# One-core MoE transformer layer: final norm spread over the last expert, one chunk for gate and up, routing lists as stationary operand

## The chip, the core and the metric

The kernel runs on one core of one Trainium2 chip. The metric is the device time in microseconds (us). Before the change it is 2897.74 us, the median of 3 runs (2894.93 to 2900.19). The engines are TensorE (PE; PEld is its weight load), VectorE (DVE), ScalarE (ACT), GpSimd (POOL) and SyncE (SP), which issues most transfers.

## What is computed

A transformer layer of 1024 tokens of width 1024: modulated RMS norm, attention, Fourier and pooling mixers, merge, output projection; then a mixture of 16 experts in which each expert chooses 128 tokens, and a final RMS norm. The change touches only the end:

```python
affinity = jax.nn.softmax((h @ w_router).astype(jnp.float32), axis=-1)
gates, idx = lax.top_k(jnp.swapaxes(affinity, 1, 2), cap)        # 16 experts, cap = 128 tokens
xg = h[b_idx, idx]
a = jnp.einsum('becd,edf->becf', xg, w_gate)                     # d = 1024, f = 2816
u = jnp.einsum('becd,edf->becf', xg, w_up)
y = jnp.einsum('becf,efd->becd', jax.nn.silu(a) * u, w_down) * gates[..., None]
out = jnp.zeros_like(h).at[b_idx, idx].add(y)
...
x = x + g2 * out
return rmsnorm(x, final_norm_g)
```

## The kernel before

Everything up to the experts stays as it is. The function `moe` (L1071) streams the weights of 16 experts, 34.6 MB each, through SBUF. The 2816 hidden columns are cut into chunks of 512, the last (c = 5) of 256. The unit of work is a **half**: half of one chunk's gate, up or down matrix, 1 MB (0.5 MB in the last chunk). An expert is 36 halves, in the order gate, up, and the down of the chunk before: g0 g1 u0 u1 | g0 g1 u0 u1 d0 d1 | ... The list `halves` holds them all, and one loop runs over them. In its turn j it does, in this order:

- what was put into `before[j]`;
- `products(j)`: 12 matmuls of 512 columns (three for each 128-deep slice, `mm3`, L70). In the last chunk gate and up have 12 matmuls of 256 columns for each half, and down has 6 of 512;
- after u1, `gated` (L1205): the product of Silu(gate) and up on DVE; its transposes (`turn`, L1209) are put two turns later;
- `split(j + 4)` (L1167): a cast of the raw half on ACT (L67) and a subtraction on DVE (L68) give the high and low parts in a `whl` buffer. There are four of these, so the cast waits for the products of turn j;
- `load(j + 15)` (L1154): SP issues the transfer into the next of 12 raw buffers, once the split that read that buffer is done;
- after g1, `silu` (L1201) on ACT.

The order on PE, ACT and DVE is this program's order, written out by hand; each engine works through its queue in order, and so do SP and POOL.

In the third chunk (c = 2) of an expert the next expert's tokens are chosen. `choose_hot` (L1095) builds a 0/1 matrix on DVE after g0; before u1 `choose_rows` (L1104) multiplies it, as stationary operand, with a table of four columns (L1109, 8 matmuls), and DVE copies token numbers and gate out of PSUM (L1112, L1118, L1119). POOL then gathers the rows (L1114), and PE transposes them in c = 4. The result of an expert is scaled (`scaled`, L1218) and added into `xacc` in DRAM by a scatter on POOL (L1226) in the next expert's second chunk.

The last expert is not scattered. `final` (L1304) loads the 8 blocks of 128 tokens of `xacc`, builds a 0/1 matrix `hot`, splits the scaled result, adds it into the blocks with 32 matmuls, squares each block on ACT (L1339), takes the reciprocal root (`rstd`, L103), multiplies and stores 8 blocks (L1350).

Of the kernel before, what the change touches and what calls it, by code (L numbers as in the profile page):

```python
# [19 lines left out]
D = 1024  # L20
# [18 lines left out]
class Kernel:  # L39
# [63 lines left out]
    def rstd(self, ss, pool, tag):  # L103
# [967 lines left out]
    def moe(self, upto):  # L1071
        nc, io = self.nc, self.io
        NR = RING
        with ExitStack() as st:
# [3 lines left out]
            ring_pool("wraw3", 5)  # L1078
            ring_pool("wraw4", NR - 8 - 3)
# [5 lines left out]
            cnt = [0]  # L1085

            class Ring:
                def tile(_, *a, **k):
                    cnt[0] += 1
                    return raws[(cnt[0] - 1) % NR].tile(*a, **k)  # L1090

            ring = Ring()
# [11 lines left out]
            def choose_rows(ex, held=None):  # L1104
# [3 lines left out]
                for c in range(CB):  # L1108
                    nc.tensor.matmul(tp[:, :4], hot[:, c], self.tv[:, c, e], start=c == 0, stop=c == CB - 1)  # L1109
# [42 lines left out]
            raw, W = {}, {}  # L1152

            def load(j):  # L1154
# [3 lines left out]
                f0, n = chunks[c]  # L1158
                if w == "w_down":
                    v, k, cols = io[w][e][f0:f0 + n], n // 256, D  # L1160
                else:
                    v, k, cols = io[w][e][:, f0:f0 + n], KT // 2, n
                v = v.rearrange("(k p) c -> p k c", p=128)[:, k * s:k * s + k]
                raw[j] = ring.tile([128, 2048], F32, name="wraw"), k, cols
                nc.sync.dma_start(raw[j][0][:, :k * cols].rearrange("p (k c) -> p k c", c=cols), v)
# [14 lines left out]
            def products(j, ex):  # L1180
                w, e, c, s = halves[j]
                n = chunks[c][1]
                hl = W.pop(j)
# [10 lines left out]
                if s == 0:  # L1194
                    ex.h[w] = psg.tile([128, 512], F32, name=w)
                for k in range(KT // 2):
                    kk = s * (KT // 2) + k
                    self.mm3(ex.h[w][:, :n], ex.xT[:, 0, kk], ex.xT[:, 1, kk], hl[:, 0, k], hl[:, 1, k],
                             kk == 0, kk == KT - 1)

            def silu(ex, n):  # L1201
                ex.a = sp.tile([128, 512], F32, name="a")
                nc.scalar.activation(ex.a[:, :n], ex.h["w_gate"][:, :n], AF.Silu)

            def gated(ex, n):  # L1205
                nc.vector.tensor_mul(ex.a[:, :n], ex.a[:, :n], ex.h["w_up"][:, :n])
                ex.ready = ex.a
# [33 lines left out]
            for j in range(9):  # L1241
                load(j)
            with self.pool("first", 1, side="right") as fp:

                ex = expert(0)
                choose_rows(ex, fp.tile([128, 6144], I32, name="first"))
            ring_pool("wraw5", 3)
            for j in range(9, NR):
                load(j)
# [6 lines left out]
            for j in range(NR, NR + AHEAD - 1):  # L1256
                load(j)
# [3 lines left out]
            for j, (w, e, c, s) in enumerate(halves):  # L1261
# [6 lines left out]
                if s == 1 and w == "w_up":  # L1268
                    gated(ex, n)
                    if c == last:  # L1270
                        split(j + AHEAD - 1)

                        put(after, j + 1, ("first", lambda ex=ex, c=c, n=n: turn(ex, c, n)))
                    else:
                        put(before, j + 2, lambda ex=ex, c=c, n=n: turn(ex, c, n))
# [4 lines left out]
                if (w, c, s) != ("w_up", last, 0):  # L1280
                    split(j + AHEAD)
                load(j + AHEAD + NR - 1)
# [3 lines left out]
                if s == 1 and w == "w_gate":  # L1286
                    silu(ex, n)
# [10 lines left out]
            for b in range(2):  # L1298
                scaled(ex, b)
            order.close()  # L1300
# [134 lines left out]
```

## Time and profile before

| | |
|---|---|
| median of 3 runs | 2897.74 us |
| the profiled execution's own time | 2896.28 us |
| its span, first to last instruction | 2894.5 us |
| PE busy | 2774.9 us (96%) |
| DVE busy | 2038.0 us (70%) |
| ACT busy | 1686.1 us (58%) |
| HBM read and written | 710 and 71 MB |

The experts take from about 1320 us to 2860 us, 95.4 us each; `final` takes the rest. In a profile row of the timeline the first number is the start in us from the span's start, the second the time to the end of the last instruction of the row; x8 means that eight instructions in a row are merged. In square brackets stands how long the engine sat idle before and who released it. PE records overlap: a matmul's pace is the distance between starts.

### The profile page before, as it was taken

The numbers are of one execution on the slowest core, as the hardware profiler recorded it, in microseconds if no ns is written. First come the engines' busy times: TensorE is split into PE (matmuls) and PEld (weight loads), VectorE is DVE, ScalarE is ACT, GpSimd is POOL, SyncE is SP. The second block draws the span as 40 slices with busy tenths as digits, with TensorE's granted clock in tenths as the row PEclk, the third lists the DMA queues.
The fourth block names the chain that finished last, engine by engine and source line by source line (L and its number), as shares of the span: only waits on it lengthen the run. The fifth ranks groups of instructions, "written<-read, shape, count | busy, mean of one in ns | idle before, by whom it ended". The sixth has DMA issues, their size and how long they took to land.

```text
span 2894.5 us, 36071 instructions
## 1 busy us (share of the span) xinstructions
PE 2774.9 (96%) x13607; PEld 2303.0 (80%) x13607; DVE 2038.0 (70%) x2412; ACT 1686.1 (58%) x2005; POOL 279.6 (10%) x436
## 2 busy tenths in 40 slices
PE   7999999999999889996999999999999999999996
PEld 3888888888788787875888888888888888888885
DVE  4423231235578773478889888998899889988997
ACT  5412121212068781244777777777777777777775
POOL 1111000000144320000000000000000000000000
PEclk9999999999999999997999999999999999999998
DMA  8434231224968748557999999999999999999994
GB/s 249 175 124 152 74 131 55 95 82 154 299 173 207 179 135 285 179 171 270 337 365 387 369 376 369 383 372 374 368 382 375 375 370 379 376 374 368 371 385 184
DMA packets 346351, 783.54 MB, mean 271 GB/s; under 512 B 17288, under 2 KB 61008, under 8 KB 346048
## 3 DMA queue, kind: packets, MB, share of 16 engines
q1 hardware_dynamic: 326272, 713.48, 70.0%
q0 software_dynamic: 19664, 67.60, 6.9%
q8 instruction: 107, 1.75, 0.3%
q14 instruction: 68, 0.56, 0.1%
q10 hardware_dynamic: 240, 0.16, 0.0%
HBM read 710.37 MB, written 70.80 MB: 270 GB/s over the span
## 4 chain that ended last, share of the span: by engine, by line
PE 45%; DMA 3%; DVE 3%; ACT 3%; issue 1%; DVEq 0%
PE y L72 5%; PE y L74 5%; PE y L73 5%; PE w_gate L74 5%; PE w_gate L72 5%; PE w_gate L73 5%; PE w_up L72 5%; PE w_up L74 4%; PE w_up L73 4%; DMA wraw<-in_w_up 3%; PE tp L1212 1%; ACT whl L67 1%; DVE whl L68 1%; ACT xT L1138 1%; DMA wraw<-in_w_down 0%
## 5 line engine op out<-in xcount | busy, mean ns | idle before, releaser
L68 DVE TENSOR_TENSOR whl<-wraw,whl 128x2048 fp32r<-128x2048 f32 (+1 forms) x656 | 1292.6, 1997 | 216.2 <-ACT whl L67 213.9
L67 ACT CAST whl<-wraw 128x2048 fp32r<-128x2048 f32 (+1 forms) x660 | 1091.1, 1671 | 414.0 <-PE y L74 124.9
L73 PE MATMUL mm<-hT,whl 128*128 128x512 f32 x768 | 301.4, 393 | 1.6 <-DVE hT L278 1.6
L72 PE MATMUL mm<-hT,whl 128*128 128x512 f32 x768 | 300.3, 392 | 1.5 <-ACT hT L272 1.5
L74 PE MATMUL mm<-hT,whl 128*128 128x512 f32 x768 | 301.2, 392 | 0.0
L74 PE MATMUL w_gate<-whl,xT 128*128 128x512 f32 (+1 forms) x768 | 286.9, 374 | 2.8 <-DVE xT L1143 2.8
L72 PE MATMUL w_gate<-whl,xT 128*128 128x512 f32 (+1 forms) x768 | 289.5, 377 | 0.0
L72 PE MATMUL w_up<-whl,xT 128*128 128x512 f32 (+1 forms) x768 | 288.7, 376 | 0.0
L73 PE MATMUL w_gate<-whl,xT 128*128 128x512 f32 (+1 forms) x768 | 286.3, 373 | 0.0
L74 PE MATMUL w_up<-whl,xT 128*128 128x512 f32 (+1 forms) x768 | 286.0, 372 | 0.0
L73 PE MATMUL w_up<-whl,xT 128*128 128x512 f32 (+1 forms) x768 | 285.6, 372 | 0.0
L72 PE MATMUL y<-whl,aT 128*128 128x512 f32 x704 | 282.4, 401 | 0.0
L74 PE MATMUL y<-whl,aT 128*128 128x512 f32 x704 | 275.5, 391 | 0.0
L73 PE MATMUL y<-whl,aT 128*128 128x512 f32 x704 | 275.2, 391 | 0.0
L72 PEld LDWEIGHTS mm<-hT,whl 128*128 128x128 f32 x768 | 145.0, 189 | 37.3 <-ACT sg L534 5.2
L73 PEld LDWEIGHTS mm<-hT,whl 128*128 128x128 f32 x768 | 145.2, 189 | 31.9 <-DVE hT L278 2.1
L74 PEld LDWEIGHTS mm<-hT,whl 128*128 128x128 f32 x768 | 145.4, 189 | 30.0
L74 PEld LDWEIGHTS w_gate<-whl,xT 128*128 128x128 f32 x768 | 145.1, 189 | 29.0 <-DVE xT L1143 3.5
L73 PEld LDWEIGHTS w_gate<-whl,xT 128*128 128x128 f32 x768 | 145.4, 189 | 24.8
L74 PEld LDWEIGHTS w_up<-whl,xT 128*128 128x128 f32 x768 | 144.8, 188 | 25.6
L72 PEld LDWEIGHTS w_gate<-whl,xT 128*128 128x128 f32 x768 | 145.3, 189 | 24.7
L73 PEld LDWEIGHTS w_up<-whl,xT 128*128 128x128 f32 x768 | 144.9, 189 | 24.1
(354 smaller groups left out, 4327.9 us busy)
## 6 DMA issues: line engine op xcount, KB each, us to landing
wraw<-in_w_gate SPq DMA_DIRECT2D x160, 1024.0 KB, 11.4
wraw<-in_w_up SPq DMA_DIRECT2D x160, 1024.0 KB, 9.2
wraw<-in_w_down SPq DMA_DIRECT2D x160, 1024.0 KB, 12.0
wraw<-in_w_in SPq DMA_DIRECT2D x28, 1024.0 KB, 5.5
wraw<-in_ada_w SPq DMA_DIRECT2D x24, 1024.0 KB, 7.5
wraw<-in_w_gate SPq DMA_DIRECT2D x32, 512.0 KB, 12.4
wraw<-in_w_up SPq DMA_DIRECT2D x32, 512.0 KB, 9.4
wraw<-in_w_down SPq DMA_DIRECT2D x32, 512.0 KB, 6.3
```

Of the source, the lines that this page charges most:

```text
L67: self.nc.scalar.copy(hi, src)
L68: (eng or self.nc.vector).tensor_sub(lo, src, f(hi))
L72: mm(out, lh, rh, start=start, stop=False, **kw)
L73: mm(out, lh, rl, start=False, stop=False, **kw)
L74: mm(out, ll, rh, start=False, stop=stop, **kw)
L1138: nc.scalar.activation(ex.xT[:, 0, kk], tp[:, cs], AF.Identity, bias=B, scale=A)
L1212: nc.tensor.transpose(tp[:, 128 * k:128 * k + 128], ex.ready[:, 128 * k:128 * k + 128], self.ident)
```

## The change

Three edits. (1) The lists: `choose_list` multiplies with the table as stationary operand (4 columns) and the 0/1 matrix as moving operand (128 columns); DVE copies the 4 x 128 result to SBUF; one turn later `choose_rows` transposes it on PE and goes on as before. (2) The last chunk's gate and up columns lie side by side: two halves named "both" of 512 columns, 34 halves in an expert instead of 36; Silu and `gated` follow at once. (3) The final norm: with H halves in all, five of the 12 raw buffers are kept, from turn H-27 on, for the norm's gain and the 1024 rows of `xacc`; squares, two `rstd` of four blocks each, scalings in place and stores of all rows are spread over turns H-22 to H-4 of the last expert. The last expert gathers its own 128 rows of `xacc`; after its last matmul it adds them, norms these rows alone and scatters them over `out`. The last two halves are multiplied together, first all of one half of the columns, then the other. `final` is gone. The five kept buffers are one pool now (`wraw4`).

```diff
-    def rstd(self, ss, pool, tag):
+    def rstd(self, ss, pool, tag, eps=None):
...
+        if eps is not None:
+            nc.scalar.activation(s, ss, AF.Sqrt, scale=1.0 / D, bias=eps)
         nc.vector.tensor_scalar(v, ss, 1.0 / D, EPS, op0=ALU.mult, op1=ALU.add)
-        nc.scalar.sqrt(s, v)
+        if eps is None:
+            nc.scalar.sqrt(s, v)
...
-            ring_pool("wraw3", 5)
-            ring_pool("wraw4", NR - 8 - 3)
+            ring_pool("wraw3", 1)
+            ring_pool("wraw4", NR - 7)
...
-            def choose_rows(ex, held=None):
+            def choose_list(ex):
                 e, hot = ex.hot
                 tp = pst.tile([128, 512], F32, name="tp")
                 for c in range(CB):
-                    nc.tensor.matmul(tp[:, :4], hot[:, c], self.tv[:, c, e], start=c == 0, stop=c == CB - 1)
+                    nc.tensor.matmul(tp[:4, :128], self.tv[:, c, e], hot[:, c], start=c == 0, stop=c == CB - 1)
+                ex.list = sp.tile([4, 128], F32, name="list", bufs=1)
+                nc.vector.tensor_copy(ex.list, tp[:4, :128])
+
+            def choose_rows(ex, held=None):
+                tp = pst.tile([128, 512], F32, name="tp")
+                nc.tensor.transpose(tp[:, :4], ex.list, self.ident[:4, :4])
...
-                    todo = [("w_gate", c), ("w_up", c)] + [("w_down", c - 1)] * (c > 0) + [("w_down", c)] * (c == last)
+                    todo = [("both", c)] if c == last else [("w_gate", c), ("w_up", c)]
+                    todo += [("w_down", c - 1)] * (c > 0) + [("w_down", c)] * (c == last)
...
+            def finish_load(i):
+                t = fin[i] = ring_tile(keep=True)
...
+                    nc.sync.dma_start(t.rearrange("p (s d) -> p s d", s=2),
+                                      self.xacc[256 * (i - 1):256 * i].rearrange("(s p) d -> p s d", s=2))
...
+            def finish_square(i):
...
+                nc.scalar.activation(fin[0][:, D:], fin_row(i), AF.Square,
+                                     accum_out=fin["ss", i // 4][:, i % 4:i % 4 + 1])
...
+            def finish_store(i):
+                x = fin_row(i)
+                nc.vector.scalar_tensor_tensor(x, x, fin["r", i // 4][:, i % 4:i % 4 + 1], fin[0][:, :D],
+                                               op0=ALU.mult, op1=ALU.mult)
+                nc.sync.dma_start(io["out"][128 * i:128 * i + 128], x)
...
+            H = len(halves)
+            FIN = H - 12
...
+            late = {H - 29: [lambda ex: finish_rows(ex)]}
+            for i, lag in enumerate((22, 21, 20, 19, 17, 15, 14, 12)):
+                late.setdefault(H - lag, []).append(lambda ex, i=i: finish_square(i))
+            late.setdefault(H - 18, []).append(lambda ex: finish_rstd(0))
+            late.setdefault(H - 10, []).append(lambda ex: finish_rstd(1))
+            for i, lag in enumerate((17, 15, 14, 13, 9, 8, 7, 4)):
+                late.setdefault(H - lag, []).append(lambda ex, i=i: finish_store(i))
+
+            def stream(j):
+                if j < FIN:
+                    load(j)
+                elif j < FIN + 5:
+                    finish_load(j - FIN)
+                else:
+                    load(j - 5)
...
+                if s == 1 and w == "both":
+                    silu(ex, ex.h[w][:, :n])
+                    gated(ex, ex.h[w][:, n:2 * n])
+                    put(after, j + 1, ("first", lambda ex=ex, c=c, n=n: turn(ex, c, n)))
...
-                        put(before, j + 3, lambda nx=nxt: choose_rows(nx))
+                        put(before, j + 3, lambda nx=nxt: choose_list(nx))
+                        put(before, j + 4, lambda nx=nxt: choose_rows(nx))
...
-            self.final(psg, ex.yo, ex.gate)
...
+                for fn in late.get(j, ()):
+                    fn(ex)
+            ss = sp.tile([128, 4], F32, name="ss")
             for b in range(2):
                 cs = slice(512 * b, 512 * b + 512)
+                scaled(ex, b)
+                nc.vector.tensor_add(ex.yo[:, cs], ex.yo[:, cs], ex.xg[:, cs])
+                nc.scalar.activation(fin[0][:, D:][:, cs], ex.yo[:, cs], AF.Square, accum_out=ss[:, b:b + 1])
+            nc.vector.tensor_add(ss[:, 2:3], ss[:, 0:1], ss[:, 1:2])
+            r = self.rstd(ss[:, 2:3], sp, "rl", fin["eps"])
+            nc.vector.scalar_tensor_tensor(ex.yo, ex.yo, r, fin[0][:, :D], op0=ALU.mult, op1=ALU.mult)
+            nc.gpsimd.indirect_dma_start(
+                out=io["out"][:, :], out_offset=bass.IndirectOffsetOnAxis(ap=ex.tok, axis=0),
+                in_=ex.yo, in_offset=None)
```

## Rows read from the trace of the kernel before

**Rows 1.** Busy time by stretch: stretch, length, then busy (count) of each engine, clock, DMA.

```profile
2500.00:2700.00 200.00, 199.21 (x960) 165.91 (x959) 179.81 (x122) 154.53 (x134) 12.12 (x5) 1.00 1.02 375
```

**Rows 2.** Timeline of PE where the next expert's tokens are chosen.

```profile
2708.78 0.95 PE L1109 MATMUL tp<-tv,xg 128*128 128x4 f32 x8
2709.59 0.49 PE L72 MATMUL w_up<-whl,xT 128*128 128x512 f32 x1
...
2712.45 0.39 PE L72 MATMUL y<-whl,aT 128*128 128x512 f32 x1
```

**Rows 3.** Timeline of ACT and DVE at the same place.

```profile
2708.98 1.90 ACT L67 CAST whl<-wraw 128x2048 fp32r<-128x2048 f32 x1 [0.32 <-PE w_up L74]
...
2708.89 4.49 DVE L68 TENSOR_TENSOR whl<-wraw,whl 128x2048 fp32r<-128x2048 f32 x2
2713.30 0.15 DVE L1112 CAST tok<-tp 128x1 int32<-128x1 f32 x1
```

**Rows 4.** Groups of DVE instructions by shape: count, then busy us, mean ns.

```profile
L986 DVE COPY v<-tp 16x128 f32<-16x128 f32 x4 | 1.1, 282 | 0.9 <-PE tp L980 0.8
```

**Rows 5.** Timeline of PE: last chunk's gate and up, and 512-column products.

```profile
1704.10 0.28 PE L72 MATMUL w_gate<-whl,xT 128*128 128x256 f32 x1
...
1709.85 0.39 PE L72 MATMUL y<-whl,aT 128*128 128x512 f32 x1
...
2706.06 0.39 PE L72 MATMUL w_up<-whl,xT 128*128 128x512 f32 x1
```

**Rows 6.** Timeline of ACT and DVE in the last expert.

```profile
2804.36 1.91 ACT L67 CAST whl<-wraw 128x2048 fp32r<-128x2048 f32 x1 [0.32 <-PE w_up L74]
...
2843.41 1.05 ACT L67 CAST whl<-wraw 128x1024 fp32r<-128x1024 f32 x1 [1.67 <-PE y L74]
...
2848.03 3.71 ACT L67 CAST whl<-wraw 128x2048 fp32r<-128x2048 f32 x2 [0.39 <-PE w_gate L74]
...
2817.66 2.29 DVE L68 TENSOR_TENSOR whl<-wraw,whl 128x2048 fp32r<-128x2048 f32 x1 [0.43 <-ACT whl L67]
```

**Rows 7.** The last scatter on POOL; then transfers: count, KB, median us to landing.

```profile
2790.19 3.39 POOL L1226 DMA_INDIRECT xacc<-yo,tok  x1 [75.49 <-DVE yo L1222]
...
xacc<-yo,tok POOLq DMA_INDIRECT x11, 11.2
...
wraw<-in_w_gate SPq DMA_DIRECT2D x160, 1024.0 KB, 11.4
...
wraw<-in_w_in SPq DMA_DIRECT2D x28, 1024.0 KB, 5.5
```

**Rows 8.** Timeline of the end: last matmul, table load, and steps of `final`.

```profile
2855.74 1.28 ACT L1312 ACT_TABLE_LOAD   x1
...
2857.03 0.20 ACT L1312 ACTIVATE first<-ident 128x1 f32<-128x1 f32 x1
...
2860.14 1.43 DVE L1222 SCALAR_TENSOR_TENSOR yo<-y,gate,g2b 128x512 f32<-128x512 f32 x2 [2.74 <-PE y L74]
...
2860.39 0.39 PE L74 MATMUL y<-whl,aT 128*128 128x512 f32 x1
...
2865.00 1.06 ACT L1339 ACTIVATE o<-xt 128x1024 f32<-128x1024 f32 x1 [2.78 <-DVE xt L1337]
...
2865.97 0.18 ACT L1339 ACTIVATION_READ_ACCUMULATOR o<-xt 128x1 f32 x1
...
2871.15 1.28 DVE L1349 SCALAR_TENSOR_TENSOR o<-xt,rfr,fg 128x1024 f32<-128x1024 f32 x1
...
2882.57 0.20 ACT L111 ACTIVATE rfs<-rfv 128x2 f32<-128x2 f32 x1 [0.19 <-DVE rfv L110]
2882.80 0.17 DVE L112 RECIPROCAL rfr<-rfs 128x2 f32<-128x2 f32 x1 [0.27 <-ACT rfs L111]
```

**Rows 9.** The 8 stores of the output: issue first to last, and time to landing.

```profile
L1350 SPq DMA_DIRECT2D out<-o x8: 332/332/338, 2872.5 to 2887.9; - x8
...
DMA to landing us min/median/max: 2.6/2.6/3.0
```

More of the change, by code (lines that the diff above doesn't have):

```diff
@@ L1084, in moe, with ring_tile @@
             g2b = self.bcast(sp, self.modd[:, 3 * D:4 * D], "g2b")
[L1085 to L1092, printed above, removed]
+            slots = list(range(NR))
+            def ring_tile(keep=False):
+                i = slots.pop(0)
+                if not keep:
+                    slots.append(i)
+                return raws[i].tile([128, 2048], F32, name="wraw")
             chunks = [(512 * c, min(512, FF - 512 * c)) for c in range((FF + 511) // 512)]
@@ new lines, in moe @@
+            late.setdefault(H - 18, []).append(lambda ex: finish_rstd(0))
[7 more added lines that the diff above has]
+                    finish_load(j - FIN)
+                else:
+                    load(j - 5)
@@ L1158, in load @@
                 f0, n = chunks[c]
+                k, cols = (n // 256, D) if w == "w_down" else (KT // 2, 512)
+                raw[j] = ring_tile(), k, cols
+                to = raw[j][0][:, :k * cols].rearrange("p (k c) -> p k c", c=cols)
+                part = lambda a: a.rearrange("(k p) c -> p k c", p=128)[:, k * s:k * s + k]
                 if w == "w_down":
-                    v, k, cols = io[w][e][f0:f0 + n], n // 256, D
-                else:
[L1162 to L1165, printed above, removed]
+                    nc.sync.dma_start(to, part(io[w][e][f0:f0 + n]))
+                elif w == "both":
+                    for i, m in enumerate(("w_gate", "w_up")):
+                        nc.sync.dma_start(to[:, :, n * i:n * i + n], part(io[m][e][:, f0:f0 + n]))
+                else:
+                    nc.sync.dma_start(to, part(io[w][e][:, f0:f0 + n]))
             def split(j, step=2048):
@@ L1182, in products @@
                 n = chunks[c][1]
+                if j == H - 2:
+                    return
+                if j == H - 1:
+                    for b in range(2):
+                        bs = slice(512 * b, 512 * b + 512)
+                        for kk in range(n // 128):
+                            k, hl = kk % (n // 256), W[H - 2 + kk // (n // 256)]
+                            self.mm3(ex.y[b], ex.aT[c][:, 0, kk], ex.aT[c][:, 1, kk], hl[:, 0, k, bs], hl[:, 1, k, bs],
+                                     False, kk == n // 128 - 1)
+                    return
                 hl = W.pop(j)
@@ L1194, in products, with silu, gated @@
                 if s == 0:
[L1195 removed]
+                    ex.h[w] = psg.tile([128, 512], F32, name="w_up" if w == "w_up" else "w_gate")
                 for k in range(KT // 2):
                     kk = s * (KT // 2) + k
[L1198 removed]
+                    self.mm3(ex.h[w], ex.xT[:, 0, kk], ex.xT[:, 1, kk], hl[:, 0, k], hl[:, 1, k],
                              kk == 0, kk == KT - 1)
[L1201 removed]
+            def silu(ex, gate):
+                n = gate.shape[1]
                 ex.a = sp.tile([128, 512], F32, name="a")
[L1203 to L1206 removed]
+                nc.scalar.activation(ex.a[:, :n], gate, AF.Silu)
+            def gated(ex, up):
+                n = up.shape[1]
+                nc.vector.tensor_mul(ex.a[:, :n], ex.a[:, :n], up)
                 ex.ready = ex.a
@@ L1248, in moe @@
             for j in range(9, NR):
-                load(j)
+                stream(j)
             split(0, 1024)
@@ L1256, in moe @@
             for j in range(NR, NR + AHEAD - 1):
-                load(j)
+                stream(j)
             before, after = {}, {}
@@ L1268, in moe @@
                 if s == 1 and w == "w_up":
[L1269 to L1275, printed above, removed]
+                    gated(ex, ex.h[w])
+                    put(before, j + 2, lambda ex=ex, c=c, n=n: turn(ex, c, n))
+                if s == 1 and w == "both":
+                    silu(ex, ex.h[w][:, :n])
+                    gated(ex, ex.h[w][:, n:2 * n])
+                    put(after, j + 1, ("first", lambda ex=ex, c=c, n=n: turn(ex, c, n)))
                 todo = after.pop(j, [])
@@ L1279, in moe @@
                         fn()
-                if (w, c, s) != ("w_up", last, 0):
-                    split(j + AHEAD)
-                load(j + AHEAD + NR - 1)
+                split(j + AHEAD)
+                stream(j + AHEAD + NR - 1)
                 for kind, fn in todo:
```

70 lines of the change are left out of this document (20 added, 50 removed).

## The prediction

> **What bounds the kernel now.** I read the busy times by stretch first. In a stretch in the middle of the experts PE is busy for 199.2 of 200 us at the full granted clock [rows 1]: what shortens or lengthens PE's queue there counts in full, 15 or 16 times. DVE (179.8) and ACT (154.5) have little room and much room, and all the same no wait of theirs reaches PE. Then the timeline, at three places: where the next tokens are chosen [rows 2, 3], where the last chunk runs [rows 5], and from the last expert to the end [rows 6, 8, 9]. After the last matmul, issued at 2860.39 [rows 8], the span runs on to 2894.5: a tail of 34.1 us with PE nearly idle. So two things can change: PE's queue within an expert, and the tail, which the change pays for with more work in the last expert.
>
> **Part 1, gate and up side by side.** 48 matmuls of 256 columns took 1709.85 - 1704.10 = 5.75 us [rows 5], 0.12 us each. Twelve of 512 columns took 2708.78 - 2706.06 = 2.72 us [rows 2, 5], 0.227 each, so the 24 that take their place take 5.44. That is -0.31 us for each expert, on PE's queue: -4.6 us for experts 0 to 14 (the last is in part 3). Silu and the gated product now follow the last matmul of the pair; the transposes that wait for them stand 2.72 us later, and both steps (below 0.6 us each, at 256 columns) end well before. Nothing for that.
>
> **Part 2, the lists.** Today the 8 matmuls hold PE from 2708.78 to the next product at 2709.59, 0.81 us; the products of u1 end at 2712.45 [rows 2]. How fast the turned matmuls are needn't be settled, because something else comes last. The change makes PE wait for a DVE copy of the list before the next turn, and that copy takes the place in DVE's queue where the token copy L1112 stands today: behind the subtraction of turn u0's split. The matmuls of that turn end at 2708.78; the cast that waits for them runs from 2708.98 to 2710.88; the subtraction ends with the pair at 2713.38; L1112 starts at 2713.30, 4.5 us after the list's matmuls were issued [rows 3]. The new copy has 128 columns out of PSUM; the nearest row is 0.28 us for 16 x 128 [rows 4]. So the list stands in SBUF at 2713.58, and with about 0.15 us (an estimate) for the hand-over and the one transpose, the first product of d0 starts at 2713.75 instead of 2712.45: **+1.3 us**. If the list's matmuls are faster, PE just waits longer. Behind the waiting transpose stands all of PE's queue, and as PE is the bound, nothing gives the time back. Bounds: 1.0 (copy of 0.15, as L1112, and no hand-over) and 1.45. Fifteen choices are made in the loop: 15 x 1.3 = +19.5 us (15 to 21.7). Before expert 0 the list is made once on a clear DVE; a copy and a transpose more and a shorter run of matmuls: 0, within 0.5. The gather moves one turn later; its rows are needed nine turns (over 24 us) after, which covers it.
>
> **Part 3, the last expert.** DVE and ACT get the norm's work while they split weights. For ACT take the 14 turns H-22 to H-9: their casts start at 2804.36 and end with the start of the one at 2843.41 [rows 6], 39.1 us. The work: 14 casts, 1.80 us apart back to back (3.71 for two [rows 6]) = 25.2; 8 squares of 1.06 + 0.18 [rows 8] = 9.9; two Silu and two casts of the transposed product, 0.6 each (the 512-wide DVE step has 0.7 [rows 8]) = 2.4; two roots = 0.4; three table loads of 1.28 [rows 8], since Silu and the root need different tables, = 3.8. Sum 41.7: ACT ends 2.6 us late, and squares stand ahead of casts. The first square also waits for its rows: they may be read only when expert 14's scatter has landed, 2790.19 + 11.2 = 2801.4 [rows 7], plus 5.5 for a transfer of 1 MB on a queue that has run empty (as w_in's [rows 7]) = 2806.9, where the square could start at 2806.2: 0.7 more.
>
> For DVE take everything from the subtraction at 2817.66 [rows 6] to the last one: 12 subtractions at 2.2 (4.49 for two [rows 3]) = 26.4, two half-wide ones 2.4, two `rstd` of six steps 0.2 apart [rows 8] = 2.4, seven scalings at 1.25 (1.28 each [rows 8]) = 8.8, three gated products and two `aT` subtractions, 0.4 to 0.6 each, = 2.8. Sum 42.8, so it ends at 2860.5 even if it never waits. Without delay PE would start the last 12 products at 2860.39 - 11 x 0.227 - 0.31 = 2857.6 and need that subtraction three matmuls later, 2858.3: at least 2 us late. Walking the three queues turn by turn with these prices, I find DVE kept waiting for late casts, and PE late at the transposes that wait for gated products, which stand in DVE's queue behind them: about 3.9 us in chunk 3, 2.0 in chunk 4, 1.0 in chunk 5. So +6.9 us, and with the 0.31 in it nothing more (bounds 1.8, only the sum above, and 10, one more turn lost). The weights come in time: with 7 buffers left a load is issued 14.8 us before its cast, against 11.4 to landing [rows 7]; the 4.2 MB of `xacc` start when the queue is empty, and PE's own delay widens the room. SP, which waits for the scatter with the `xacc` load, holds back loads that aren't due for 20 us. Part of the stores stand ahead of loads on SP, in turns in which the load has 8 us or more.
>
> **Part 4, the tail.** L is the issue of the last matmul, 2860.39 before. The second column half is ready for DVE 0.43 us later (today DVE starts 0.43 after the first half's last matmul, three issues before L [rows 8]). Then scaling 0.7, adding 0.7, hand-over 0.1, square of 512 columns 0.6 and its read-out 0.18, sum of both halves beside a table load of 1.28, root 0.20, five small steps 1.0, scaling 1.28, hand-over to POOL 0.3: L + 6.8. The first half runs before it. The scatter without addition isn't in the trace. Bounds: 2.6 us, a plain store of the same 0.5 MB [rows 9], and 11.2, the adding scatter among weight loads [rows 7]. I take 4.8, near the plain store, since nothing else is in the queue then and POOL needs some 2 us to issue. After the last landing today (2887.9 + 2.6 to 3.0 [rows 9]) 3.8 us pass to the span's end; they stay. Sum L + 15.4, instead of L + 34.1: **-18.7 us** (-20.9 to -12.3). The Trainium skill, "DMA: Bandwidth & Descriptors", Anatomy of one DMA, gives 2.0 us plus bytes / 436 GB/s for a transfer issued by GpSimd, 3.2 us here as an estimate; the gather and scatter of this trace landed far later, and by the page the sum would be 1.6 us lower.
>
> **The sum.** -4.6 + 19.5 + 6.9 - 18.7 = +3.1 us. On the profiled execution that is 2896.28 + 3.1 = 2899.4 us (its span is 2894.5, 1.8 lie around it); it ran 1.5 us below the median of the three runs. On the median: 2897.74 + 3.1 = 2900.8. Bounds added up reach from -8 to +16. A difference under 0.2%, 5.8 us, is about what can't be told from none.
>
> **The rivals.**
> - *The list costs PE nothing.* If the copy reached DVE 1.1 us earlier than L1112 does today, or the wait were absorbed, part 2 falls away: 2881. Against it: the place in the queue is the one whose start the trace shows. 0.14.
> - *The last expert is covered.* The three queues lose only the 1.8 us of the DVE sum: 2895.7. For it: DVE runs four turns ahead at the start. 0.15.
> - *Slower, at the `xacc` rows.* The squares stand in ACT's queue ahead of casts. If the first rows land with a loaded queue's 11.4 us instead of 5.5 [rows 7], at 2812.8, every cast behind is 5.9 us later, and DVE and PE with it: 2907. It decides from 2.7 us on, at landings after 2809.6. Against it: the queue has had nothing new for 10 us. 0.17.
> - *Slower, at the table loads.* If a switch cost ACT 1.4 us more than its row, four in the last expert and one in the tail would cost up to 7 us more: 2907. The trace has the root 0.01 us after the load ends [rows 8], which speaks against it. The Trainium skill, "ScalarE: Activation LUTs", What ACT_TABLE_LOAD costs, adds a drain of about 1.38 us to each switch; by that rule this is the case. 0.04.
> - *The ring of 7 buffers starves.* Landings of 15 us or more in the last expert would stop PE for several us: 2909. 0.03.
>
> **How the numbers follow.** My forecast has 0.47: 2900.8, on its own 2894 to 2907 (0.02 faster, 0.35 same, 0.10 slower). Faster: 0.02 + 0.14 + 0.05 of the covered case = 0.21. Same: 0.35 + 0.10 = 0.45. Slower: 0.10 + 0.17 + 0.04 + 0.03 = 0.34. The range goes from 2885 to 2911: it takes in the bounds nearly whole and leaves out most of the first rival (0.11) and the ends of the slow ones (0.06).
>
> **What will show it.** Right if PE waits for DVE's list copy 1 us or more in each expert; if experts 0 to 14 take 96.4 us instead of 95.4; if PE waits for gated products in the last expert; if the tail is about 15 us. The prediction is wrong if the list's transpose starts without a wait, or if the last expert's delay lies outside 2 to 10 us.

## The result, and the profile after

The changed kernel takes 2915.26 us, the median of 4 runs (2911.68 to 2918.03), beside 2898.97 for the kernel before: a ratio of 1.0058 (95% interval 1.0045 to 1.0070). It is slower by 16 us, where +3.1 was forecast, and lies above the range. The profiled execution ran for 2915.62 us, 2913.8 of it the span, 19.3 more than the span of before.

The gathers and scatters on POOL cut the span into its parts. Timeline of POOL after: the last two adding scatters of the experts, and the one that now ends the kernel.

```profile
2724.98 3.39 POOL L1313 DMA_INDIRECT xacc<-yo,tok  x1 [74.31 <-DVE yo L1309]
...
2822.32 3.39 POOL L1313 DMA_INDIRECT xacc<-yo,tok  x1 [74.31 <-DVE yo L1309]
...
2905.08 0.97 POOL L1398 DMA_INDIRECT out<-yo,tok  x1 [68.92 <-DVE yo L1396]
```

The last matmul, timeline of PE after:

```profile
2898.23 0.39 PE L74 MATMUL y<-whl,aT 128*128 128x512 f32 x1
```

An expert takes 97.34 us from scatter to scatter; before it took 95.40 (2694.80 to 2790.19, the last one in [rows 7]). The first gather of the experts starts 3.2 us later than in the trace of before (1325.50 and 1322.33). The code ahead of it is the same, and in the runs below that start lies anywhere from 1318.8 to 1326.7, so those 3.2 us are not the change's. From there to the scatter of expert 14 it is 1496.8 us instead of 1467.9. The last matmul is issued at 2898.23, 75.9 us behind that scatter (70.2 before), and the span ends 15.6 us after it (34.1 before).

| stretch | forecast | measured |
|---|---|---|
| ahead of the experts | 0 | +3.2 (same code) |
| experts 0 to 14 | +14.9 | +29.0 |
| expert 15, scatter of 14 to last matmul | +6.9 | +5.7 |
| tail | -18.7 | -18.5 |
| sum | +3.1 | +19.4 (19.3 from span to span, the rest is rounding) |

So one term is far off: an expert grew by 1.94 us, not by 1.0. Busy time by stretch, after, the stretch of [rows 1]: PE now idles for 5.3 of 200 us, at the full clock.

```profile
2500.00:2700.00 200.00, 194.72 (x896) 159.49 (x895) 173.84 (x116) 150.02 (x128) 8.73 (x4) 1.00 1.01 368
```

What PE waited for from 1700 to 2600 us (us in total, times, longest), first before and then after:

```profile
PE tp L1212 <- DVE a L1206: 4.0, 10, 0.4
```

```profile
PE tp L1120 <- DVE list L1115: 12.5, 9, 1.4
PE tp L1299 <- DVE a L1293: 12.4, 10, 1.2
```

There are two waits, not one. The first is the list's. Timeline of PE and DVE after, at the place of [rows 2, 3]:

```profile
2738.97 0.66 PE L1113 MATMUL tp<-xg,tv 128*4 128x128 f32 x8
...
2743.82 0.22 PE L1120 MATMUL tp<-ident,list 4*128 4x4 f32 x1 [1.38 <-DVE list L1115]
2743.97 0.50 PE L72 MATMUL y<-whl,aT 128*128 128x512 f32 x1
...
2746.85 0.60 PE L1299 MATMUL tp<-ident,a 128*128 128x128 f32 x4
...
2739.09 4.49 DVE L68 TENSOR_TENSOR whl<-wraw,whl 128x2048 fp32r<-128x2048 f32 x2
2743.49 0.27 DVE L1115 COPY list<-tp 4x128 f32<-4x128 f32 x1
```

The copy starts 4.5 us after the list's matmuls, behind the two subtractions, and PE stands for 1.38 us. From the list's first matmul to the first product of d0 it is 5.00 us, where it was 3.67 before [rows 2]. The twelve products behind the wait then take 2.88 us up to the next transposes, 0.15 more than the 2.73 of before (2712.45 [rows 2] to this row of PE before):

```profile
2715.18 0.60 PE L1212 MATMUL tp<-ident,a 128*128 128x128 f32 x4
```

The second wait was there before, at 0.39 us, and has become 1.25: PE's transposes of chunk 4's gated product. Timeline of ACT, DVE and PE at that place, before and then after:

```profile
2744.94 1.09 ACT L67 CAST whl<-wraw 128x1024 fp32r<-128x1024 f32 x1
...
2748.85 0.69 DVE L1143 TENSOR_TENSOR xT<-a,xT 128x512 fp32r<-128x512 f32 x1 [0.80 <-ACT a L1142]
2749.47 0.68 DVE L1206 TENSOR_TENSOR a<-a,w_up 128x512 f32<-128x512 f32 x1
...
2750.29 0.63 PE L1212 MATMUL tp<-ident,a 128*128 128x128 f32 x4 [0.39 <-DVE a L1206]
```

```profile
2776.61 1.95 ACT L67 CAST whl<-wraw 128x2048 fp32r<-128x2048 f32 x1
...
2781.38 0.69 DVE L1154 TENSOR_TENSOR xT<-a,xT 128x512 fp32r<-128x512 f32 x1 [0.51 <-ACT a L1153]
2781.99 0.68 DVE L1293 TENSOR_TENSOR a<-a,w_up 128x512 f32<-128x512 f32 x1
...
2782.82 0.63 PE L1299 MATMUL tp<-ident,a 128*128 128x128 f32 x4 [1.25 <-DVE a L1293]
```

The cast in that turn splits a half of the last chunk. With gate and up side by side the half is 2048 wide, and the cast takes 1.95 us instead of 1.09. It stands in ACT's queue ahead of the eight steps of `turned` for the next expert; DVE's subtraction for these (L1143, L1154) comes ahead of the gated product, and PE waits for that: 0.86 us more. An expert's account by the waits: 1.39 (list) + 0.86 - 0.31 (merged matmuls) = 1.94, what was measured. That it fits to the hundredth is luck: a wait's idle time is not quite its price, as the list's shows, and each edit by itself costs 1.47 and 0.48 (below).

### The profile page after: what moved, and what is told of

The parts are those of the page before. It is cut to its first block, busy times and chain, and to the rows that moved or that the text cites. A ratio compares the mean times of both kernels' runs of the same rounds, so it can differ in the third digit from the quotient of the medians.

```text
span 2913.8 us, 35119 instructions
## 1 busy us (share of the span) xinstructions
PE 2764.2 (95%) x13207; PEld 2274.0 (78%) x13207; DVE 2032.4 (70%) x2378; ACT 1682.8 (58%) x1974; POOL 275.7 (9%) x436
## 4 chain that ended last, share of the span: by engine, by line
PE 39%; DVE 9%; DMA 7%; ACT 4%; issue 4%; POOLq 0%; DVEq 0%; ACTq 0%; SPq 0%
DMA wraw<-in_w_gate 6%; DVE whl L68 6%; PE y L72 4%; PE w_gate L74 4%; PE y L74 4%; PE w_gate L72 4%; PE w_gate L73 4%; PE y L73 4%; PE w_up L74 2%; PE w_up L73 2%; PE w_up L72 2%; ACT whl L67 2%; PE mm L72 2%; PE mm L73 2%; PE mm L74 2%
## 5 line engine op out<-in xcount | busy, mean ns | idle before, releaser
L74 PE MATMUL w_gate<-whl,xT 128*128 128x512 f32 x768 | 300.1, 391 | 2.8 <-DVE xT L1154 2.8
L72 PE MATMUL w_gate<-whl,xT 128*128 128x512 f32 x768 | 302.7, 394 | 0.0
L73 PE MATMUL w_gate<-whl,xT 128*128 128x512 f32 x768 | 299.6, 390 | 0.0
L72 PE MATMUL w_up<-whl,xT 128*128 128x512 f32 x640 | 251.6, 393 | 0.0
L74 PE MATMUL w_up<-whl,xT 128*128 128x512 f32 x640 | 249.4, 390 | 0.0
L73 PE MATMUL w_up<-whl,xT 128*128 128x512 f32 x640 | 249.1, 389 | 0.0
L1313 POOL DMA_INDIRECT xacc<-yo,tok x15 | 50.8, 3387 | 1114.6 <-DVE yo L1309 1114.6
L74 PEld LDWEIGHTS y<-whl,aT 128*128 128x128 f32 x704 | 132.6, 188 | 29.2
```

The costliest lines, as they stand in the source:

```text
L72: mm(out, lh, rh, start=start, stop=False, **kw)
L73: mm(out, lh, rl, start=False, stop=False, **kw)
L74: mm(out, ll, rh, start=False, stop=stop, **kw)
L1313: nc.gpsimd.indirect_dma_start(out=self.xacc[:, :], out_offset=bass.IndirectOffsetOnAxis(ap=ex.tok, axis=0), in_=ex.yo, in_offset=None, co ...
```

## The experiments

"Period" is the mean time from scatter to scatter over experts 0 to 14, "end" the time from the last adding scatter to the end of the span; both come from one profile. Each ratio is to runs of the kernel before that were made beside it; their medians lie between 2896.38 and 2898.97 us.

| kernel | median us | ratio (95%) | period | end |
|---|---|---|---|---|
| before | 2897.74 | | 95.40 | 104.3 |
| after | 2915.26 | 1.0058 (1.0045 to 1.0070) | 97.34 | 91.5 |
| list_alone | 2918.06 | 1.0074 (1.0058 to 1.0091) | 96.87 | 104.3 |
| both_alone | 2903.92 | 1.0020 (1.0008 to 1.0031) | 95.88 | 103.7 |
| list_later | 2891.86 | 0.9981 (0.9971 to 0.9990) | 95.80 | 92.3 |
| turn_later | 2899.66 | 1.0008 (0.9999 to 1.0018) | 96.07 | 94.3 |
| both_later | 2875.07 | 0.9922 (0.9905 to 0.9939) | 94.55 | 95.7 |
| list_old_turn_later | 2877.43 | 0.9939 (0.9923 to 0.9956) | 94.64 | 92.6 |
| no_norm_edit | 2884.17 | 0.9956 (0.9942 to 0.9970) | 94.57 | 103.7 |
| eased | 2881.93 | 0.9950 (0.9934 to 0.9967) | 94.57 | 98.8 |
| late_root_alone | 2915.91 | 1.0064 (1.0048 to 1.0081) | 97.32 | 91.4 |
| late_root | 2872.07 | 0.9910 (0.9894 to 0.9927) | 94.54 | 91.4 |
| last_turn_kept | 2872.18 | 0.9921 (0.9904 to 0.9937) | 94.54 | 92.3 |
| split_root | 2870.94 | 0.9906 (0.9890 to 0.9923) | 94.54 | 90.7 |

**Each of the two edits alone, on the kernel before.** list_alone takes the hunks of `choose_list` and `choose_rows`, both_alone those of `todo`, `load`, `products`, `silu` and `gated`, with the order of the splits that goes with them.

```diff
+                        put(before, j + 3, lambda nx=nxt: choose_list(nx))
-                        put(before, j + 3, lambda nx=nxt: choose_rows(nx))
+                        put(before, j + 4, lambda nx=nxt: choose_rows(nx))
```

> The kernel before with edit 1 alone: the lists as stationary operand (128-column list, copy to SBUF, 4-column transpose one turn later); gate and up of the last chunk, and the final norm, stay as they were. Theory (the prediction's Part 2): TensorE waits some 1.4 us for VectorE's copy of the list in each of the 15 experts that choose a successor, as the trace of after shows at the transpose of the list (1.39 us each), and nothing is given back elsewhere: an expert takes 95.40 + 1.39 = 96.8 us and the time rises by some 20 us, to about 2919. Rival (the prediction's first rival): the wait only takes the place of one that stood later, the period stays at 95.4 and the time within some 5 us of before.

```diff
-                    todo = [("w_gate", c), ("w_up", c)] + [("w_down", c - 1)] * (c > 0) + [("w_down", c)] * (c == last)
+                    todo = [("both", c)] if c == last else [("w_gate", c), ("w_up", c)]
+                    todo += [("w_down", c - 1)] * (c > 0) + [("w_down", c)] * (c == last)
```

> The kernel before with edit 2 alone: the last chunk's gate and up columns in one tile of 2 x 256 columns, with the half splits that go with it. Theory formed on the trace of after: the half that is split in the turn ahead of the next expert's second set of transposes is 2048 wide and not 1024, ScalarE's cast takes 1.95 us and not 1.09, and all that stands behind it comes 0.86 us later: the wait of TensorE for the gated product of chunk 4 grows from 0.39 to about 1.25 us an expert; against this the 0.31 us saved at the matmuls: +0.55 us an expert, a period of 95.95 us, and about +8 us in all. Rival (the prediction's Part 1): the edit costs nothing elsewhere, -0.31 us an expert, a period of 95.1 us and -5 us in all, and the growth of that wait in after came from the list edit or from the two edits together.

Waits of PE from 1700 to 2600 us, list_alone and then both_alone:

```profile
PE tp L1116 <- DVE list L1111: 12.4, 9, 1.4
PE tp L1219 <- DVE a L1213: 4.0, 10, 0.4
```

```profile
PE tp L1219 <- DVE a L1213: 12.6, 10, 1.3
```

Each edit brings its own wait and leaves the other alone. The list costs 1.47 us an expert, the merged columns 0.48 (0.55 was expected); 1.47 + 0.48 = 1.95 is the change's 1.94. The rival of both_alone, that the wait grew by the list edit or by the two edits together, falls, and so does the prediction's "nothing for that": by itself the merged chunk makes the kernel slower.

**Each wait taken away from the changed kernel**, by putting the step that waits one turn later:

```diff
-                        put(before, j + 4, lambda nx=nxt: choose_rows(nx))
+                        put(before, j + 5, lambda nx=nxt: choose_rows(nx))
```

> The changed kernel with the transpose of the list (and the gather's issue behind it) put one turn later. Theory: the list is long copied by then, TensorE's wait of 1.39 us for it goes and nothing is late in its place: the period falls from 97.34 to about 95.95 us, the time by some 20 us. Rival: the gather of the next expert's rows starts a turn of some 3.5 us later and its rows come too late for the next expert's transposes, so that a wait for the gather takes the place of the one for the list; the period then stays within 0.5 us of 97.34.

```diff
-                    put(before, j + 2, lambda ex=ex, c=c, n=n: turn(ex, c, n))
+                    put(before, j + 2 + (c == 4), lambda ex=ex, c=c, n=n: turn(ex, c, n))
```

> The changed kernel with only the turning of chunk 4's gated product put one turn later; the list's transpose stays where the change put it. Theory: only the wait for that product goes (1.25 us an expert), the list's 1.39 us stays: a period of about 96.1 us. In the last expert the moved step costs some 4 us, as the trace of both_later showed (3.6 us of TensorE's wait for the turned columns and then slower matmuls), so 2915 - 19 + 4 = about 2900 us. Rival: the two waits hang together, and without the list's edit out of the way the period stays above 96.7 us.

> The changed kernel with two steps put one turn later: the transpose of the list, and the turning of chunk 4's gated product. Theory: both waits go, 1.39 and 1.25 us an expert; the 0.31 us of the merged matmuls and the old 0.39 us wait of chunk 4 stay as gains, a period of about 94.7 us, 15 x 2.64 = some 40 us below the changed kernel, about 2876 us, under both kernels. Rival: the turn to which chunk 4's transposes go is already full on ScalarE or VectorE, the w_down products behind them wait instead, and no more than the list's 1.39 us an expert (some 20 us) is won.

Waits of PE from 1700 to 2600 us, list_later and then turn_later; both_later has none in that stretch:

```profile
PE tp L1299 <- DVE a L1293: 12.7, 10, 1.3
```

```profile
PE tp L1120 <- DVE list L1115: 12.5, 9, 1.4
```

The list's turn gives back 1.53 us an expert (0.14 more than its wait, about the 0.15 that the products behind the wait lost), chunk 4's turn 1.27, and both together 2.79: they are independent, and in experts 0 to 14 nothing is late in their place. The gather, which list_later issues a turn later too, makes nobody wait. both_later is faster than both kernels. Its last expert has a new wait, though (timeline of PE):

```profile
2847.31 0.79 PE L74 MATMUL y<-whl,aT 128*128 128x512 f32 x1 [3.63 <-DVE aT L68]
```

There the moved turn stands right ahead of its reader, with the norm's products between. last_turn_kept moves it only where a successor follows (the edit against both_later):

```diff
-                    put(before, j + 2 + (c == 4), lambda ex=ex, c=c, n=n: turn(ex, c, n))
+                    put(before, j + 2 + (c == 4 and e + 1 < NE), lambda ex=ex, c=c, n=n: turn(ex, c, n))
```

> both_later with chunk 4's turning left at its old place in the last expert alone. Theory: the wait of TensorE for the turned columns in the last expert of both_later (3.6 us and slower matmuls behind it) comes from the moved step, which there stands right ahead of its reader: the last expert is that of after again, some 91.5 us from the last scatter-add to the end instead of 95.6, and the time about 2871. Rival: that wait comes from the products with the root in VectorE's queue wherever the turning stands: 94 us or more, and the time stays at 2875.

That wait is gone and the end is 92.3 us, as expected. That the end is shorter for it is not shown: the intervals of the times overlap, and turn_later and list_old_turn_later (below), whose last expert has the same code as both_later's, end after 94.3 and 92.6 us. Their waits at the same place, turn_later and then list_old_turn_later:

```profile
PE y L74 <- DVE aT L68: 2.3, 1, 2.3
```

```profile
PE y L74 <- DVE aT L68: 2.1, 1, 2.1
```

So an end read from one profile is good to some 3 us where the turn is moved in the last expert. Where it is not (after, list_later, last_turn_kept) the ends are 91.5 to 92.3. Part of the spread is TensorE's clock: turn_later and list_old_turn_later had slow matmuls behind the wait in chunk 3, both_later had none there and came to the second wait earlier. Its stretches behind the two waits (of 3.29 us up to 2817.56, and of 3.63 us up to 2847.31):

```profile
2815.00:2820.00 5.00, 2.44 (x13) 2.09 (x14) 5.00 (x4) 5.00 (x5) 0.00 (x0) 1.00 1.01 406
2820.00:2825.00 5.00, 5.00 (x24) 4.13 (x23) 5.00 (x5) 3.91 (x5) 0.00 (x0) 1.00 1.09 358
...
2845.00:2850.00 5.00, 2.69 (x6) 2.15 (x7) 4.85 (x6) 0.00 (x0) 0.00 (x0) 0.65 0.36 139
```

**What the list edit and the norm edit are worth with the waits gone.** list_old_turn_later takes the lists as the kernel before does, beside turn_later's edit; no_norm_edit is the kernel before with both other edits and both moved turns.

> The changed kernel with the lists taken as in the kernel before (the one-hot columns as stationary operand, one step, no copy of a list) and the turning of chunk 4's gated product one turn later. Theory: with its wait out of the way the list edit is worth almost nothing either way, since eight 4-column matmuls and eight 128-column ones take nearly the same: a period within 0.25 us of the 94.55 us of both_later, and a time within 4 us of its 2875. Rival (what the edit is for): the eight loads of 128 stationary columns cost TensorE 0.5 us or more, the period is 95.0 us or longer and the time some 8 us above both_later.

> The kernel before with edits 1 and 2, the list's transpose and the turning of chunk 4's product each one turn later, and the final norm as it was, behind the last expert. Theory: the experts' period is the 94.55 us of both_later, the tail is the old one, 34 us instead of 15.5, and the last expert has no added work and takes some 70 us instead of 80: the time is 8 to 12 us above both_later, some 2884 us, and the norm edit as it stands is worth about 9 to 13 us and not its tail's 18.5. Rival (the prediction's second rival): the work spread over the last expert is covered, and the norm edit is worth the whole 18 us: about 2893 us.

The list edit alone saves 0.09 us an expert (94.64 to 94.55), 1.4 in all, which the times don't tell from nothing. The norm edit, as it stands in both_later, is worth 2884.17 - 2875.07 = 9.1 us, by the profiles' ends 103.7 - 95.7 = 8.0, and with the turn kept 12.0 by the times and 11.4 by the ends. That is what the theory said, and the rival of 18 falls: the tail's 18.5 us are paid for with 6 to 10 in the last expert (76.6 us from the last adding scatter to the last matmul in last_turn_kept, 80.0 in both_later, 69.9 in no_norm_edit). By the periods, the merged columns with the 0.39 us wait of before gone are worth the rest: 95.40 - 94.64 = 0.76 us an expert, of which 0.39 is the old wait.

**The last expert.** In after it waits three times, 3.8 us together; the first and longest, timeline of PE:

```profile
2858.33 0.39 PE L74 MATMUL y<-whl,aT 128*128 128x512 f32 x1
2861.41 0.66 PE L1299 MATMUL tp<-ident,a 128*128 128x128 f32 x4 [2.69 <-DVE a L1293]
2861.82 0.58 PE L72 MATMUL y<-whl,aT 128*128 128x512 f32 x1
...
2862.62 0.63 PE L74 MATMUL y<-whl,aT 128*128 128x512 f32 x1
2863.05 0.63 PE L72 MATMUL y<-whl,aT 128*128 128x512 f32 x1
...
2865.55 0.40 PE L72 MATMUL y<-whl,aT 128*128 128x512 f32 x1
```

After the wait nine matmuls run 0.41 us apart on the mean (2861.82 to 2865.55) instead of 0.227: 1.7 us more. Is it the norm's work in the queues of ACT and DVE? late_root_alone spaces the squares two turns apart, takes one root for all rows behind the last silu, and puts the products behind it, four of them behind the final scatter:

```diff
-            for i, lag in enumerate((22, 21, 20, 19, 17, 15, 14, 12)):
+            for i, lag in enumerate((22, 20, 18, 16, 14, 12, 10, 8)):
...
-            late.setdefault(H - 18, []).append(lambda ex: finish_rstd(0))
-            late.setdefault(H - 10, []).append(lambda ex: finish_rstd(1))
-            for i, lag in enumerate((17, 15, 14, 13, 9, 8, 7, 4)):
+            late.setdefault(H - 4, []).append(lambda ex: finish_rstd())
+            for i, lag in enumerate((3, 2, 2, 1)):
...
+            for i in range(4, 8):
+                finish_store(i)
```

In this kernel and in late_root, which adds last_turn_kept's two moves to it, the four stores behind the scatter cover its rows, so the last expert's share of the rows of those four tiles is left out of the output.

> The changed kernel with only its last expert rearranged: the eight squares two turns apart instead of one, one root for all eight row tiles behind the last silu (so that the tail's own root finds its table loaded: three table loads of 1.28 us fewer), the products with the root in the last three turns (four tiles) and behind the tail's last product (four tiles), all on VectorE. The experts before are those of after. Theory (the prediction's Part 3): what the norm puts ahead of the gated products in ScalarE's and VectorE's queues is the whole loss of the last expert, 5.7 us, the slow matmuls after the wait included: from the last scatter-add to the end 91.5 - 5.7 - 1.3 = some 84.5 us, no matmul at 0.43 us, and a time of about 2908. Rival: the wait of chunk 3 comes from the traffic of the row tiles beside the weights, or from the squares themselves: the stretch stays at 89 us or more and the time at about 2914.

> late_root_alone with the list's transpose one turn later and the turning of chunk 4's product one turn later in the experts that have a successor (the last one keeps its old place), so the three waits that the traces of after showed are all taken away. Theory: a period of 94.55 us, 84.5 us from the last scatter-add to the end, about 2863 us: some 11 us below both_later and 35 below the kernel before, which is what the three edits are worth with their waits gone (the list 1.4, the merged columns 12, the norm some 20). Rival: the last expert's waits only move (to the last chunk, or to the stores behind the end): 2870 us or more.

Busy time by stretch (stretch, length, busy and count of PE, PEld, DVE, ACT, POOL, then clock, DMA share, GB/s), after and then late_root_alone:

```profile
2861.40:2864.00 2.60, 2.59 (x10) 2.12 (x11) 2.60 (x2) 2.60 (x3) 0.00 (x0) 0.62 1.03 396
2864.00:2868.00 4.00, 4.00 (x16) 3.28 (x15) 4.00 (x3) 2.15 (x4) 0.00 (x0) 0.82 1.09 351
```

```profile
2861.40:2864.00 2.60, 2.60 (x13) 2.16 (x12) 2.17 (x3) 2.23 (x2) 0.00 (x0) 1.00 1.05 370
2864.00:2868.00 4.00, 4.00 (x20) 3.30 (x19) 3.68 (x2) 3.67 (x4) 0.00 (x0) 1.00 1.09 349
```

Without the wait there is no fall of the clock, with the same transfers running (DMA share over 1 in all four). From the last adding scatter to the last matmul it is now 69.86 us (2821.98 to 2891.84), the 70.20 of before less the merged chunk's 0.31. So the last expert's loss lies all in how the norm's steps stand in the two queues; the row tiles' transfers, which are the same, and eight squares two turns apart cost nothing. How much of it the closer squares, the two earlier roots and the earlier products each cost was not separated. This half of the theory held. The forecast of the time did not: what was won came back in the tail, 21.6 us instead of 15.6, in both kernels. Timeline of DVE, POOL and SP at late_root_alone's end:

```profile
2889.85 4.87 DVE L1195 SCALAR_TENSOR_TENSOR wraw<-wraw,rfr 128x1024 f32<-128x1024 f32 x4
2894.64 0.75 DVE L1308 SCALAR_TENSOR_TENSOR yo<-y,gate,g2b 128x512 f32<-128x512 f32 x1
...
2901.34 1.77 POOL L1397 DMA_INDIRECT out<-yo,tok  x1 [65.19 <-DVE yo L1395]
...
2905.51 2.86 SPq L1197 DMA_DIRECT2D out<-wraw  x4
```

The four products ahead hold the last expert's own rows up until 2894.64, 2.8 us after the last matmul (0.9 before it in after): +3.7. The table is loaded already: -1.1 from there to the scatter. The last four stores wait for the scatter to land and go out at 2905.51: +3.3. Together +5.9, where 21.6 - 15.6 = 6.0 was measured. So late_root's rival held, the waits move to the end; the rival of late_root_alone had the time right and its cause wrong.

split_root tries the middle: one root for six tiles behind chunk 3's gated product, one for two tiles behind the last silu, all stores ahead of the scatter, and last_turn_kept's moves.

```diff
-            late.setdefault(H - 18, []).append(lambda ex: finish_rstd(0))
-            late.setdefault(H - 10, []).append(lambda ex: finish_rstd(1))
-            for i, lag in enumerate((17, 15, 14, 13, 9, 8, 7, 4)):
+            late.setdefault(H - 15, []).append(lambda ex: finish_rstd(0))
+            late.setdefault(H - 4, []).append(lambda ex: finish_rstd(1))
+            for i, lag in enumerate((14, 13, 11, 9, 7, 6, 2, 1)):
```

> The list's transpose and chunk 4's turning one turn later (the latter only in experts with a successor), and a last expert whose root for six row tiles stands behind chunk 3's gated product (two table loads of 1.28 us) and whose root for the other two stands behind the last silu, so that the tail finds its table loaded; six products with the root spread over seven turns of VectorE, two behind the last turning, and all eight stores ahead of the final scatter. Theory: the last expert loses at most 2 us of the 5.7 (VectorE has some 0.3 us free in a turn, and the gated products some 2.5 us of room), the tail is 1.28 us shorter for the table and 1.5 us longer for the last two products: 86 to 88 us from the last scatter-add to the end, a period of 94.55 us, 2863 to 2867 us in all, the fastest of all the variants. Rival: the products in chunks 4 and 5 still make TensorE wait as in after: 91 us from the last scatter-add to the end and 2870 us.

Timeline of PE, split_root's two waits of the last expert:

```profile
2817.93 0.66 PE L1301 MATMUL tp<-ident,a 128*128 128x128 f32 x4 [0.65 <-DVE a L1295]
...
2837.18 0.66 PE L1301 MATMUL tp<-ident,a 128*128 128x128 f32 x4 [2.23 <-DVE a L1295]
```

The rival was right: PE waits 0.65 us in chunk 3, but now 2.23 us in chunk 4, where one of the norm's products stands in DVE's queue two steps ahead of the gated one; the end takes 90.7 us, and the time, 2870.94, is that of last_turn_kept within the intervals. Rearranging gave 1 to 2 us by the ends, which the times don't tell from nothing.

**GpSimd instead.** eased gives the product with the norm's weights to POOL, ahead of a single root, and leaves DVE and ACT a one-operand step:

```diff
+                nc.gpsimd.tensor_mul(fin_row(i), fin_row(i), fin[0][:, :D])
...
-                nc.vector.scalar_tensor_tensor(x, x, fin["r", i // 4][:, i % 4:i % 4 + 1], fin[0][:, :D],
-                                               op0=ALU.mult, op1=ALU.mult)
+                if i < 4:
+                    nc.vector.tensor_scalar(x, x, fin["r"][:, i:i + 1], None, op0=ALU.mult)
+                else:
+                    nc.scalar.activation(x, x, AF.Identity, scale=fin["r"][:, i:i + 1])
```

> both_later with a lighter last expert: chunk 4's turning stays at its old place in that expert alone, one root for all eight row tiles instead of two (2 table loads of 1.28 us fewer, and six small VectorE steps fewer), the product with the norm's weights put on GpSimd ahead of the root, and the product with the root as a one-operand step on VectorE (four tiles) and on ScalarE (four tiles). Theory: TensorE waits in the last expert because what the norm puts in ScalarE's queue (squares and table loads, chunk 3) and in VectorE's (products of 1.28 us, chunks 4 and 5) stands ahead of the gated products: with less of it the last expert takes some 70 to 72 us instead of 80, no matmul runs at 0.43 us, and the time is about 2865 us. Rival: the waits come from the row tiles' transfers, or GpSimd's products slow VectorE's steps down by as much as they take off it: the last expert stays above 76 us and the time above 2870.

Timeline of POOL, DVE and PE in eased:

```profile
2797.03 29.33 POOL L1189 TENSOR_TENSOR wraw<-wraw 128x1024 f32<-128x1024 f32 x7 [3.46 <-ACT wraw L1187]
...
2795.40 2.29 DVE L68 TENSOR_TENSOR whl<-wraw,whl 128x2048 fp32r<-128x2048 f32 x1 [0.42 <-ACT whl L67]
...
2807.06 17.08 DVE L68 TENSOR_TENSOR whl<-wraw,whl 128x2048 fp32r<-128x2048 f32 x4
...
2824.79 1.12 PE L1301 MATMUL tp<-ident,a 128*128 128x128 f32 x4 [6.55 <-DVE a L1295]
```

The rival held, and more strongly than it said. While POOL's products run, each of DVE's four subtractions takes 4.27 us on the mean instead of 2.29, and each of POOL's seven products 4.19 instead of the 2.34 that the same shape took in no_norm_edit's tail. PE then waits 6.55 us. The work was not moved off DVE; it held DVE up. The Trainium skill, "SBUF — State Buffer", Who interferes with whom, says that an instruction of VectorE with two inputs in SBUF contends with one of GpSimd that reads SBUF; the trace agrees, with 4.2 to 4.3 us for each of a pair that alone takes 2.29 and 2.34.

## Why the prediction was wrong, step by step

- **Part 1, merged columns: the step that failed.** The saving at the matmuls was sized rightly. "Nothing for that" was not: I looked at the readers of the merged chunk (silu and the gated product of chunk 5) and not at its split, which the same edit makes twice as wide in the turns of chunk 4. The prediction's sentence that no wait of DVE or ACT reaches PE was already wrong for the kernel before: the wait list of before, shown above, has ten waits of up to 0.4 us in 900 us. The wider cast stands ahead of another step, `turned`, whose end sets a wait that the trace of before already showed at 0.39 us. Price: 0.86 us in each of 15 experts, 12.9 of the 14.1 us by which experts 0 to 14 took longer than forecast. (The two spans differ by 16.2 us more than forecast: these 14.1, 3.2 in the stretch ahead of the experts, whose code is the same, and 1.2 less in the last expert, rounded.) both_alone shows it by itself, turn_later takes it away.
- **Part 2, the lists: right.** The forecast put the first product of d0 4.97 us behind the list's matmuls, 1.3 us later than before; on the chip it is 5.00, from the place in DVE's queue that [rows 3] gave. The 0.15 us that the products behind it lost were not in the forecast; the price on the whole is 1.47 (list_alone). The first rival, "the list costs nothing", falls.
- **Part 3, the last expert: right in kind and nearly in size**, +5.7 for +6.9. The waits stand where the walk put them, in chunks 3, 4 and 5, but are 3.8 us (2.69, 0.44 and 0.70) and not 6.9; 1.7 us of matmuls at half the granted clock, which the walk did not have, made up most of the rest. That the sum came so near is in part luck. Three rivals fall: "covered", by those waits; the `xacc` rows were in time, since the first square ran at 2838.33, right behind its cast; and the ring did not starve, since no cast of the last expert waited for a transfer.
- **Part 4, the tail: right**, -18.5 for -18.7. The final scatter was issued 6.85 us after the last matmul (6.8 forecast) and landed in 3.3 us, where I took 4.8; what follows the landing is longer than the 3.8 us I took by about as much. Its row of the transfers after (count, median us to landing):

```profile
out<-yo,tok POOLq DMA_INDIRECT x1, 3.3
```

  The Trainium skill, "DMA: Bandwidth & Descriptors", Anatomy of one DMA, led to an estimate of 3.2 us, and here the trace agrees with it.
- **The table-load rival falls.** Timeline of ACT after:

```profile
2848.39 1.89 ACT L67 CAST whl<-wraw 128x2048 fp32r<-128x2048 f32 x1
2850.30 1.28 ACT L111 ACT_TABLE_LOAD   x1
2851.59 0.30 ACT L111 ACTIVATE rfs<-ss,eps 128x4 f32<-128x4 f32 x1
```

The load starts 0.02 us after the cast ends and the root 0.01 us after the load: 1.28 us is all that a switch takes from ACT. The Trainium skill, "ScalarE: Activation LUTs", What ACT_TABLE_LOAD costs, adds a drain to each switch; this trace shows none.
- **The range** took in the bounds of the costs that were named, and none for an edit that was costed at nothing: what it does to the engines that feed it. (The four terms' bounds add up to -8.7 and +14.8, not to -8 and +16; that changes nothing here.)

## What to carry to other kernels

An edit that makes a tile wider also makes everything wider that prepares the tile, in other turns: follow each of those steps to its place in its engine's queue, and ask which short wait of before stands behind it, since a wait of 0.39 us marks a chain without room. A step that waits can be moved a turn later where its reader leaves room: in 15 experts that cost nothing here, and it made the same three edits worth 23 us instead of -16; in the last expert, where the moved turn stands right ahead of its reader, it brought a wait of 2.1 to 3.6 us. Work that is spread under a busy stretch is only covered up to the room of each engine's queue there; what it delays is the short product that the bound engine waits for.

## What the runs showed of the hardware

- TensorE's clock fell in the last expert after a wait of 2.69 us: a granted clock of 0.62 in the 2.6 us behind it and 0.82 in the next 4, matmuls 0.43 us apart, which is the lower of its two levels (1.2 GHz), and 0.227 again after. The waits of 1.25 and 1.38 us in each expert left the clock at 1.00 (the stretch 2500 to 2700). The length of a single wait did not settle it: 3.29 us in both_later's chunk 3 was followed by 1.00, 2.69 us in after's by 0.62.
- GpSimd's elementwise product and VectorE's subtraction, run side by side, took 4.19 and 4.27 us, against 2.34 (POOL in no_norm_edit's tail) and 2.29 (the same subtraction while POOL is idle).
- Switching ScalarE's table cost 1.28 us, with no idle time ahead of it or behind it.
